# Cache pages in visits of four with seven buffers, late weight chunks in two sets

## The chip, the cores and the metric

The kernel is one program on one core of a Trainium2 chip. The metric is the device time of one execution in microseconds (us), taken as the median of several runs. One more execution was run with the hardware profiler; every row that is quoted comes from it.

## The reference, cut to what matters

One inference step of a two-layer decoder, for a prompt of 512 tokens and for 8 samples of 8 new tokens each. Layer 0 is a gated delta rule. Then keys and values are projected once, and layer 1 is differential attention over them. The samples also attend to 1024 older tokens each, whose keys and values lie in a paged cache: 8 pages of 128 tokens a sample, so 64 pages of keys and 64 of values.

```python
k_past = cache_k[page_table].reshape(db, past, DIFF_HEADS, 2 * DIFF_DH)
v_past = cache_v[page_table].reshape(db, past, DIFF_HEADS, DIFF_VH)
...
s = jnp.einsum('bqhmd,bkhmd->bhmqk', q, k) * DIFF_DH ** -0.5
s = jnp.where((k_pos[None, :] <= q_pos[:, None])[None, None, None], s, -jnp.inf)
p = jax.nn.softmax(s, axis=-1)
p = p[:, :, 0] - lam * p[:, :, 1]
return jnp.einsum('bhqk,bkhe->bqhe', p, v)
...
o = rms_norm(o, sub_gain) * (1.0 - lam_init)
o = o * jax.nn.silu(z.astype(F32)).reshape(b, L, DIFF_HEADS, DIFF_VH)
return o.reshape(b, L, DIFF_WIDTH).astype(h.dtype) @ w_out
```

## The kernel before, in words

The second half of the program (`phase_b`) holds layer 0's closing projection, then the projections q, k, v and z of layer 1 and the shared keys and values, the attention of prompt and samples, and the closing projection of layer 1. All 576 tokens (512 of the prompt, 64 of the samples) are columns, in two halves of 288.

**Weights.** A projection goes by chunks of 128 output rows: chunks 0 to 7 close layer 0, 8 to 15 are q, 16 to 23 k, 24 to 31 v, 32 to 39 z, 40 to 47 close layer 1. A chunk is loaded as it is (`raw`, two buffers, line 2003, on SyncE's queue) and split (`split_w`) into a rounded part `hi`, copied by ScalarE (line 2018), and a rest `lo`, subtracted in two halves by GpSimd (line 2024; half of it by VectorE for chunks 8 to 19). A chunk's half takes 24 matmuls: hi times the high part of the input, hi times its low part, lo times its high part, for 8 slices of the contraction (`run_part`). A pair hi and lo is a weight set; its room is named. Chunks up to 23 use room `w` (four sets), chunk 26 room `wx`, the other late ones `w2`: two sets, and a third from the point `late` on, when the buffers that k and q needed are given up. A set is freed behind the last matmul of its chunk's second half. In `tile_row` the first two tiles of k and z and the last two of every kind go half by half in turn (tile 6 half 0, tile 7 half 0, tile 6 half 1, tile 7 half 1); the others go one chunk after the other.

**Cache pages.** `Pages.loads` brings the 128 pages in one fixed order (keys of samples 0 to 2, then values of sample 0, keys of 3, values of 1, and so on) into a ring of `PG` = 5 buffers, 512 KB each. For each, GpSimd copies the page's number into the buffer (line 2478) once the buffer is free, SyncE reads it from there (line 2481) and issues the transfer (line 2483). `Sample2.keys` and `Sample2.values` are the users: TensorE multiplies two pages at a visit, in the form 128x32 (four column strips of the array, 16 instructions a page in the records). A half of the keys' scores (4 pages) lies in one PSUM buffer, and is copied out before the next half; the values of 8 pages add up in another. Between keys and values of a sample stands its softmax.

**The order.** A planner (`Second.drive`) writes the order of every engine while the program is built. Each piece of work is a generator with a rank; each of its steps names an engine, a cost, and what it waits for. The planner takes the step that can start first, and among equals the lowest rank: split 4, page loads 9, samples 20 to 27, prompt heads 29 and 30, projections 1000. So the projections fill TensorE where nothing else is ready. It has its own clock for the engines and the transfers. A buffer that is left inside a step counts as free at the end of that step:

```python
            for where, name in self.later:
                where[name] = end
```

The order so found is pinned for TensorE, ScalarE, VectorE, GpSimd and SyncE (`pin`): on the chip each engine takes its instructions in just this order, and waits where data are not there.

**The end.** `samples_end` joins the samples' results when all pages are done: four TensorE steps with small steps of VectorE, ScalarE and GpSimd between, then the gate with z (`gated2`). `out_second` closes layer 1: its first four half chunks are run for seven of eight slices (`HELD`), then their last slices, then the other twelve. Half 0 needs the prompt's heads alone, half 1 the samples too.

Of the kernel before, what the change touches and what calls it, by code (L numbers as in the profile page):

```python
# [10 lines left out]
F32 = mybir.dt.float32  # L11
# [17 lines left out]
NPG = 8  # L29
# [841 lines left out]
PG = 5  # L871
# [18 lines left out]
PAGES_AT = 1, 7  # L890
HELD = 4
EV = 3
CH = 3
PB = 3

# [1087 lines left out]
def act(n, k=0):  # L1983
    return 0.155 + 0.00086 * n + 0.1 * (k > 0) + 0.195 * (k > 1)
# [10 lines left out]
def weights(W, K, first, n, slot):  # L1995


    for j in range(first, first + n):
        room = "w" if j < 24 else "wx" if j == 26 and EV > 2 else "w2"
        yield None, 0, Room("raw")  # L2000
        rr, = W.took
        raw = K.wraw.tile([128, 8, 128], F32, name="wraw")
        K.nc.sync.dma_start(out=raw[:], in_=K.wall[K.worder[K.wnext + j]].rearrange("p (k m) -> p k m", m=128))
        if j <= 2:
            W.done[("raw", j)] = 0.0, None
        else:
            W.load("S", 1.5, "raw", j)
        W.add(4, split_w(W, K, j, raw, rr, room, slot[room]))


def split_w(W, K, j, raw, rr, room, slot):
    nc = K.nc
    yield "A", act(1024), ("raw", j), Room(room), *((("wa", j - 1),) if j - 1 in W.sets and j > 1 else ())
    took, = W.took
    phi, plo = slot(took[1])
    hi = phi.tile([128, 8, 128], F32R, name="whi")
    lo = plo.tile([128, 8, 128], F32R, name="wlo")
    nc.scalar.copy(out=hi[:], in_=raw[:])  # L2018
    W.sets[j] = hi, lo, took
    W.set("wa", j)  # L2020
    for q in range(0, 8, 4):
        shared = q and HALF[0] <= j < HALF[1]
        yield ("S", dve(512)) if shared else ("P", pool_op(512))
        (nc.vector if shared else nc.gpsimd).tensor_sub(out=lo[:, q:q + 4], in0=raw[:, q:q + 4], in1=hi[:, q:q + 4].bitcast(F32))  # L2024
    W.leave(rr)
    W.set("w", j)
# [320 lines left out]
def second_projections(W, K):  # L2347
# [40 lines left out]
    for i, (m, half) in enumerate(order):  # L2388
        if i < 3:
            bank = early[i][2]  # L2390
            yield from run_part(W, K, m, bank[0], half, (6, 7), conds=heads_in)
        else:
            yield from one(m, m, half, "o", nothing)
            bank = W.done_bank
        if half:
            W.leave(W.sets[m][2])
        yield None, 0, ("xl", half, m)
        W.add(0, first_out(W, K, m, m, half, xs[half, m][0], bank, xs[half, m][1]))
        if (m, half) == (7, 0):
            W.add(-6, second_norm(W, K, 0))  # L2400
        if (m, half) == (7, 1):
            W.add(-6, second_norm(W, K, 1))
# [12 lines left out]
            yield from run_part(W, K, 8 + t.h, bank[0], 1, (k,), conds=conds[1])  # L2415
    for t, bank in zip(tiles, banks):
        W.add(0, t.evac(1, bank))
        W.leave(W.sets[8 + t.h][2])
# [17 lines left out]
def tile_row(W, K, tiles, j, kind, conds, first=0):  # L2436


    order = [(t, half) for t in tiles[first:6] for half in range(2)]
    if kind in "kz":  # L2440
        order = [(t, half) for half in range(2) for t in tiles[:2]] + order[4:]
    order += [(t, half) for half in range(2) for t in tiles[6:]]
    for t, half in order:
        name = "pp" if kind in "qk" or t.h < EV and kind == "v" else "pq"
        if kind == "v" and t.h == EV and half == 0:
            yield None, 0, ("late",)
        yield from take(W, K, pick(W, "pq", "pt2", "sc", "pv") if kind == "z" and ("pv", 7, 3) in W.done else name)
        bank, = W.out
        yield from run_part(W, K, j + t.h, bank[0], half, range(8), conds=conds[half])
        W.add(0, t.evac(half, bank))  # L2450
        if half:
            W.leave(W.sets[j + t.h][2])
            if j + t.h in (20, 21, 22):
                W.leave(("w2", j + t.h - 20) if j + t.h < 22 else ("wx", 0))
        if t.h == 7:
            W.set(kind + "p", half)


class Pages:


    def __init__(self, W, K):
        self.W, self.K = W, K
        self.tiles = {}
        self.order = [("k", b) for b in range(PB)]
        for b in range(NB):
            self.order += [("v", b)] + ([("k", b + PB)] if b + PB < NB else [])

    def loads(self):
        W, K, P = self.W, self.K, self.W.P  # L2470
        nc = K.nc
        for kind, b in self.order:
            for pg in range(NPG):
                yield "Q", 0.2, Room("pg"), ("ptt",), ("sq", *PAGES_AT)
                i = b * NPG + pg
                t = K.pg.tile([128, 8, 128], F32, name="pg")
                e = t[0:1, 0, 0:1].bitcast(I32)
                nc.gpsimd.tensor_copy(out=e, in_=P.ptt[0:1, i:i + 1])  # L2478
# [4 lines left out]
                nc.sync.dma_start(out=t[:], in_=cache[bass.ds(r, 1)].rearrange("a p (h t) -> p (a h) t", h=8))  # L2483
                W.load("S", 1.55, kind + "page", i)


class Sample2:
# [5 lines left out]
    def keys(self):  # L2493
# [12 lines left out]
        p = self.p = P.sp.tile([128, 1088], F32, name="sp", bufs=PB)  # L2506
        nc.gpsimd.memset(p[:, 1024:], NEG)
        for half in range(2):
            for pair in range(2):
                ids = [b * NPG + 4 * half + 2 * pair + i for i in range(2)]  # L2510
                yield "E", None, *[("kpage", i) for i in ids], *((Room("px"),) if pair == 0 else ())
                if pair == 0:
                    sr, = W.took
                    S = K.px.tile([128, 512], F32, name="px")
                for n, i in enumerate(ids):
                    kp, kr = self.G.tiles["k", i]
                    o = 128 * (2 * pair + n)
# [65 lines left out]
    def values(self):  # L2583
        W, K, P, b = self.W, self.K, self.W.P, self.b
        nc = K.nc
        for pair in range(4):
            ids = [b * NPG + 2 * pair + i for i in range(2)]
            yield "E", None, *[("vpage", i) for i in ids], *((Room("po"),) if pair == 0 else ())
            if pair == 0:
                por, = W.took  # L2590
                po = K.po.tile([128, 4, 128], F32, name="po")
            for n, i in enumerate(ids):
                vp, vr = self.G.tiles["v", i]
                pg = 2 * pair + n
                for hf in range(2):
                    for j in range(4):
                        h = 4 * hf + j
# [19 lines left out]
def samples_end(W, K):  # L2617
# [11 lines left out]
    W.leave(xr)  # L2629
    yield "A", 0.65, Room("pg")  # L2630
    r0, = W.took
    sq = K.pg.tile([128, 8, 128], F32, name="pg")[:].rearrange("p a b -> p (a b)")[:, 0:512]
# [156 lines left out]
def out_second(W, K):  # L2789
# [40 lines left out]
    for (m, half), bank in zip(order[:HELD], held):  # L2830
        yield from run_part(W, K, 40 + m, bank[0], half, (7,), conds=conds(half))
        W.add(0, evac(m, half, bank))
        if half:
            W.leave(W.sets[40 + m][2])
    for i, (m, half) in enumerate(order[HELD:]):
        name = names[(i + HELD) % 8]
        yield None, 0, Room(name)
# [1 line left out]
        yield from run_part(W, K, 40 + m, bank[0], half, range(8), conds=conds(half))  # L2839
        W.add(0, evac(m, half, bank))  # L2840
        if half:
            W.leave(W.sets[40 + m][2])


def ada_later_loads(W, K, kts, bufs, ns, at):
# [117 lines left out]
def phase_b(K, ctx, past):  # L2963
# [41 lines left out]
    W.taken["w2"], W.taken["wx"] = 3, 1  # L3005
    W.sets[0] = *K.wq.pop(0), ("w", 0)
    W.done[("w", 0)] = max(0.0, past.done[("w", past.last)][0] - past.free["E"]), None
    own = K.whi, K.wlo
    pages = Pages(W, K)
# [3 lines left out]
    slot = {"w": lambda i: own if i % 4 < 2 else qx, "w2": lambda i: own if i % 3 < 2 else P.third, "wx": lambda i: qx}  # L3013
# [196 lines left out]
```

## Time and profile before

| | us |
|---|---|
| median of 3 runs | 1165.18 |
| lowest, highest run | 1161.04, 1165.52 |
| time of the profiled execution | 1162.21 |
| its span, first to last instruction | 1160.5 |
| TensorE busy | 1131.4 |
| VectorE, ScalarE, GpSimd busy | 690.6, 692.3, 437.7 |

The profiled execution's own time is 1.7 us above its span. TensorE appears as PE (matmuls) and PEld (weight loads), VectorE as DVE, ScalarE as ACT, GpSimd as POOL, SyncE as SP. A matmul's row begins when it starts; rows of matmuls that follow each other overlap, so the distance from start to start tells what one costs, not its own length. A row `x32` is 32 instructions of one kind in a run.

### The profile page before, as it was taken

How to read it: one execution, taken by the hardware profiler on the slowest of the kernel's cores; microseconds unless marked ns; L12 is line 12 of the kernel's file. 1: busy time of each engine (PE TensorE's matmuls, PEld its weight loads, DVE VectorE, ACT ScalarE, POOL GpSimd, SP SyncE). 2: the span in 40 equal slices, each digit the busy share in tenths (PEclk: the TensorE clock that was granted, in tenths of full speed). 3: DMA queues.
4: the chain of work that ended last, by engine and by line, in shares of the span. 5: the costliest groups of instructions: out<-in, count | busy, mean ns of one | idle time of the engine just before them, and what ended most of it. 6: DMA issues, size and time to landing. Idle time of an engine off the chain costs nothing.

```text
span 1160.5 us, 32592 instructions
## 1 busy us (share of the span) xinstructions
PE 1131.4 (97%) x12715; PEld 1039.0 (90%) x12715; DVE 690.6 (60%) x1739; ACT 692.3 (60%) x1901; POOL 437.7 (38%) x752
## 2 busy tenths in 40 slices
PE   8999999999999999999999999999999999999998
PEld 6899998989989998998989999999997887778998
DVE  4677875767877674866743757574424445554342
ACT  3675867777777767676653334775535656555320
POOL 3443434233333333232223431579933232233341
PEclk8999999999999999999999999999999999999999
DMA  9796666757657665676885888222689989898243
GB/s 365 207 230 167 147 193 134 201 146 201 167 153 171 157 199 134 190 204 149 244 248 157 304 274 322 92 74 75 231 290 309 313 310 303 300 320 282 63 137 110
DMA packets 87643, 239.96 MB, mean 207 GB/s; under 512 B 14451, under 2 KB 28659, under 8 KB 87491
## 3 DMA queue, kind: packets, MB, share of 16 engines
q1 hardware_dynamic: 71938, 181.27, 46.0%
q0 software_dynamic: 15552, 56.63, 22.4%
q8 instruction: 100, 1.64, 0.6%
q14 instruction: 53, 0.43, 0.1%
HBM read 212.02 MB, written 25.84 MB: 205 GB/s over the span
## 4 chain that ended last, share of the span: by engine, by line
PE 80%; DMA 6%; ACT 5%; issue 3%; DVE 3%; POOL 2%; SPq 0%; POOLq 0%; ACTq 0%; DVEq 0%
PE pp L271 23%; PE pp L1927 14%; PE pc L271 7%; PE pq L1927 6%; PE px L1927 4%; PE pa L271 3%; PE po L1927 3%; DMA whi<-wall 3%; PE pt L271 3%; PE sc L1927 3%; PE pt L1927 3%; PE pt L1932 3%; PE pv L1927 2%; PE ps L271 2%; PE pt L285 1%
## 5 line engine op out<-in xcount | busy, mean ns | idle before, releaser
L271 PE MATMUL pp<-hlo,whi 128*128 128x288 f32 x592 | 170.7, 310 | 0.0
L271 PE MATMUL pp<-hhi,whi 128*128 128x288 f32 x592 | 162.0, 295 | 0.0
L2024 POOL TENSOR_TENSOR wlo<-wraw,whi 128x512 fp32r<-128x512 f32 x82 | 110.1, 1359 | 113.1 <-ACT whi L2018 104.9
L1927 PE MATMUL pp<-hhi,whi 128*128 128x288 f32 x432 | 133.2, 309 | 0.7 <-DVE x L1826 0.7
L1927 PE MATMUL pp<-hlo,whi 128*128 128x288 f32 x432 | 127.3, 295 | 0.0
L1927 PE MATMUL pp<-hhi,wlo 128*128 128x288 f32 x432 | 125.8, 295 | 0.0
L271 PE MATMUL pp<-hhi,wraw 128*128 128x288 f32 x576 | 124.1, 299 | 0.0
L271 PEld LDWEIGHTS pp<-hlo,whi 128*128 128x128 f32 x592 | 111.6, 189 | 1.8 <-issue 1.4
L271 PEld LDWEIGHTS pp<-hhi,whi 128*128 128x128 f32 x592 | 111.7, 189 | 0.4
L271 PE MATMUL pp<-hhi,wlo 128*128 128x288 f32 x592 | 104.1, 304 | 0.0
L271 PEld LDWEIGHTS pp<-hhi,wraw 128*128 128x128 f32 x576 | 94.4, 189 | 1.0 <-issue 0.4
L1131 DVE SCALAR_TENSOR_TENSOR y<-u,vec,y 128x600 f32<-128x600 f32 x96 | 80.9, 842 | 10.8 <-ACT y L1128 10.2
L1927 PEld LDWEIGHTS pp<-hhi,whi 128*128 128x128 f32 x432 | 81.5, 189 | 5.2 <-issue 4.7
L271 PEld LDWEIGHTS pp<-hhi,wlo 128*128 128x128 f32 x592 | 85.1, 190 | 0.8 <-issue 0.2
L2478 POOL COPY pg<-ptt 1x1 int32<-1x1 int32 x128 | 27.5, 222 | 154.0 <-PE px L1927 67.8
L271 PE MATMUL pp<-hlo,wraw 128*128 128x288 f32 x288 | 84.7, 316 | 0.2 <-DVE hlo L1852 0.2
L1927 PEld LDWEIGHTS pp<-hlo,whi 128*128 128x128 f32 x432 | 81.6, 189 | 0.0
L1927 PEld LDWEIGHTS pp<-hhi,wlo 128*128 128x128 f32 x432 | 80.9, 189 | 0.0
L923 POOL DMA_DIRECT2D wlo<-wall x36 | 32.2, 895 | 122.4 <-ACT wlo L918 80.9
L2018 ACT CAST whi<-wraw 128x1024 fp32r<-128x1024 f32 x47 | 49.0, 1047 | 40.0 <-DMA wraw<-wall 20.1
L1927 PE MATMUL pq<-hhi,whi 128*128 128x288 f32 x192 | 61.9, 322 | 1.6 <-DVE x L2230 1.0
L1927 PE MATMUL pq<-hhi,wlo 128*128 128x288 f32 x192 | 56.7, 295 | 0.0
(483 smaller groups left out, 3135.5 us busy)
## 6 DMA issues: line engine op xcount, KB each, us to landing
pg<-ck SPq DMA_DIRECT2D x64, 512.0 KB, 5.1
pg<-cv SPq DMA_DIRECT2D x64, 512.0 KB, 4.9
wraw<-wall SPq DMA_DIRECT2D x49, 512.0 KB, 4.3
wraw<-wall POOLq DMA_DIRECT2D x36, 512.0 KB, 5.9
whi<-wall POOLq DMA_DIRECT2D x36, 512.0 KB, 5.8
wlo<-wall POOLq DMA_DIRECT2D x36, 512.0 KB, 5.7
araw<-ada SPq DMA_DIRECT2D x24, 512.0 KB, 4.3
araw<-ada SPq DMA_DIRECT2D x8, 1024.0 KB, 13.2
```

Source lines behind the costliest of these rows:

```text
L271: return self.K.nc.tensor.matmul(**kw)
L285: return self.K.nc.tensor.transpose(**kw)
L923: K.nc.gpsimd.dma_start(out=lo[:], in_=src, accum_op=ALU.add)
L1131: nc.vector.scalar_tensor_tensor(out=y[:, :YW], in0=u[:, j:j + YW], scalar=cw[j], in1=y[:, :YW], op0=ALU.mult, op1=ALU.add)
L1927: return self.K.nc.tensor.matmul(**kw)
L1932: return self.K.nc.tensor.transpose(**kw)
L2018: nc.scalar.copy(out=hi[:], in_=raw[:])
L2024: (nc.vector if shared else nc.gpsimd).tensor_sub(out=lo[:, q:q + 4], in0=raw[:, q:q + 4], in1=hi[:, q:q + 4].bitcast(F32))
L2478: nc.gpsimd.tensor_copy(out=e, in_=P.ptt[0:1, i:i + 1])
```

## The change

Samples from the fourth on (`b >= PB`) take four pages of keys at a visit in place of two, and all samples take four pages of values. The ring of page buffers has five places up to the point `late` and seven after it: two more (`MORE`) in a pool of their own, `bpg2`, which lies where the third weight set lay. That set is gone, so late chunks have two. Chunk 40, the first of the closing projection, has its set in two page buffers: its split waits for all page loads to be issued (`loads`) and for two free places of the ring. `Pages.tile` finds the pool to which a place of the ring belongs. Since chunks after 40 skip one turn in `w2`, 41 takes the set of 38 and 42 that of 39.

```diff
+BURST = 4
+MORE = 2
+OVER = 40,
...
-        room = "w" if j < 24 else "wx" if j == 26 and EV > 2 else "w2"
+        room = "w" if j < 24 else "wx" if j == 26 and EV > 2 else "pg" if j in OVER else "w2"
...
 def split_w(W, K, j, raw, rr, room, slot):
     nc = K.nc
-    yield "A", act(1024), ("raw", j), Room(room), *((("wa", j - 1),) if j - 1 in W.sets and j > 1 else ())
-    took, = W.took
-    phi, plo = slot(took[1])
-    hi = phi.tile([128, 8, 128], F32R, name="whi")
-    lo = plo.tile([128, 8, 128], F32R, name="wlo")
+    yield ("A", act(1024), ("raw", j), *((Room(room),) if slot else (Room(room), Room(room), ("loads",))),
+           *((("wa", j - 1),) if j - 1 in W.sets and j > 1 else ()))
+    took = W.took
+    if slot:
+        phi, plo = slot(took[0][1])
+        hi = phi.tile([128, 8, 128], F32R, name="whi")
+        lo = plo.tile([128, 8, 128], F32R, name="wlo")
+    else:
+        hi, lo = (W.pages.tile(r)[:].bitcast(F32R) for r in W.took)
...
+    def tile(self, room):
+        n = room[1] - self.grown
+        pool = self.K.pg2 if n >= 0 and n % (PG + MORE) < MORE else self.K.pg
+        return pool.tile([128, 8, 128], F32, name="pg")
...
         for half in range(2):
-            for pair in range(2):
-                ids = [b * NPG + 4 * half + 2 * pair + i for i in range(2)]
+            many = BURST if b >= PB else 2
+            for pair in range(4 // many):
+                ids = [b * NPG + 4 * half + many * pair + i for i in range(many)]
...
-        for pair in range(4):
-            ids = [b * NPG + 2 * pair + i for i in range(2)]
+        for pair in range(NPG // BURST):
+            ids = [b * NPG + BURST * pair + i for i in range(BURST)]
...
-                       ("w", 4), ("w2", 3), ("wx", 1), ("qs", 2), ("p", PB), ("pTs", 1), ("os", 1), ("C", 2), ("ls", 2), ("mx", 2),
+                       ("w", 4), ("w2", 2), ("wx", 1), ("qs", 2), ("p", PB), ("pTs", 1), ("os", 1), ("C", 2), ("ls", 2), ("mx", 2),
...
-    P.third = [pool(n, 1) for n in ("bwh", "bwl")]
-    W.done[("late",)] = W.left["w2", 2] = W.now, None
+    K.pg2 = pool("bpg2", MORE)
+    pages.grown = W.taken["pg"]
+    W.bufs["pg"] += MORE
+    W.done[("late",)] = W.now, None
```

More of the change, by code (lines that the diff above doesn't have):

```diff
@@ L2395, in second_projections @@
         if half:
-            W.leave(W.sets[m][2])
+            W.leave(*W.sets[m][2])
         yield None, 0, ("xl", half, m)
@@ L2451, in tile_row @@
         if half:
-            W.leave(W.sets[j + t.h][2])
+            W.leave(*W.sets[j + t.h][2])
             if j + t.h in (20, 21, 22):
@@ L2463, in __init__ @@
         self.W, self.K = W, K
-        self.tiles = {}
+        self.tiles, self.grown = {}, math.inf
         self.order = [("k", b) for b in range(PB)]
@@ L2484, in loads @@
                 W.load("S", 1.55, kind + "page", i)
+        W.set("loads")
 class Sample2:
@@ L2516, in keys @@
                     kp, kr = self.G.tiles["k", i]
-                    o = 128 * (2 * pair + n)
+                    o = 128 * (many * pair + n)
                     for hh in range(2):
@@ L2833, in out_second @@
         if half:
-            W.leave(W.sets[40 + m][2])
+            W.leave(*W.sets[40 + m][2])
     for i, (m, half) in enumerate(order[HELD:]):
@@ L2841, in out_second @@
         if half:
-            W.leave(W.sets[40 + m][2])
+            W.leave(*W.sets[40 + m][2])
 def ada_later_loads(W, K, kts, bufs, ns, at):
@@ L3004, in phase_b @@
     W.taken["pg"] = W.taken["w"] = 1
-    W.taken["w2"], W.taken["wx"] = 3, 1
-    W.sets[0] = *K.wq.pop(0), ("w", 0)
+    W.taken["w2"], W.taken["wx"] = 2, 1
+    W.sets[0] = *K.wq.pop(0), [("w", 0)]
     W.done[("w", 0)] = max(0.0, past.done[("w", past.last)][0] - past.free["E"]), None
     own = K.whi, K.wlo
-    pages = Pages(W, K)
+    pages = W.pages = Pages(W, K)
     samples = [Sample2(W, K, pages, b) for b in range(NB)]
@@ L3012, in phase_b @@
     W.add(7, set_up(W, K, one))
-    slot = {"w": lambda i: own if i % 4 < 2 else qx, "w2": lambda i: own if i % 3 < 2 else P.third, "wx": lambda i: qx}
+    slot = {"w": lambda i: own if i % 4 < 2 else qx, "w2": lambda i: own, "wx": lambda i: qx}
     W.add(3, weights(W, K, 1, 47, slot))
```

10 lines of the change are left out of this document (5 added, 5 removed).

## The prediction

> **What bounds the kernel now.** I read the shares of the page first, then TensorE's own waits, then the timeline around single page visits, the ring of page buffers, and last the chain of waits behind the last page.
>
> ```profile
> span 1160.5 us, 32592 instructions
> PE 1131.4 (97%) x12715; PEld 1039.0 (90%) x12715; DVE 690.6 (60%) x1739; ACT 692.3 (60%) x1901; POOL 437.7 (38%) x752
> ...
> PE px L1927 <- DMA pg<-ck: 1.4, 1, 1.4
> ...
> PE po L1927 <- POOL pg L2478: 0.8, 2, 0.4
> ...
> PE po L1927 <- DMA pg<-cv: 0.2, 1, 0.2
> ...
> 893.00:1077.00 184.00, 181.09 (x2575) 148.92 (x2575) 92.91 (x239) 107.75 (x315) 53.99 (x137) 1.00 0.88 301
> ...
> 893.00:1077.00 184.00, 52.72 (x1536) 38.86 (x1536) 0.00 (x0) 0.00 (x0) 19.05 (x91) 1.00 0.88 301
> ```
>
> TensorE is the bound, and nearly never idle. In its stretch of page visits, 893 to 1077 us, it is busy for 181.09 of 184 us at full clock; the last row counts there what touches pages alone: 1536 matmuls of 32 a visit, so 48 visits. All that TensorE loses on pages in the whole program is 1.4 + 0.8 + 0.2 = 2.4 us. So time can be won only where TensorE's work gets shorter, and lost only where it runs out of work.
>
> **A visit's price, and the edit to fours.**
>
> ```profile
> 1067.38 0.29 PE L1927 MATMUL pq<-hlo,whi 128*128 128x288 f32 x1
> 1067.51 0.29 PE L1927 MATMUL pq<-hhi,wlo 128*128 128x288 f32 x1
> 1067.74 1.08 PE L1927 MATMUL po<-pg,pTs 128*32 128x128 f32 x32
> 1068.75 0.40 PE L1927 MATMUL pq<-hhi,whi 128*128 128x288 f32 x1
> 1068.99 0.29 PE L1927 MATMUL pq<-hlo,whi 128*128 128x288 f32 x1
> ...
> 939.52 1.08 PE L1927 MATMUL po<-pg,pTs 128*32 128x128 f32 x32
> 940.42 0.41 PE L1927 MATMUL px<-kT,qs 128*32 128x64 f32 x16
> ...
> 984.10 0.64 PE L1932 MATMUL px<-con_ident,sp 128*128 128x128 f32 x4
> 984.67 1.08 PE L1927 MATMUL px<-pg,qs 128*32 128x128 f32 x32
> ...
> 1044.38 0.66 PE L1932 MATMUL px<-con_ident,sp 128*128 128x128 f32 x4
> 1044.88 1.06 PE L1927 MATMUL pv<-vn,pts 128*128 128x128 f32 x8
> ```
>
> Projection matmuls start 0.13 us apart (1067.38, 1067.51). Into a visit it is 0.23, from its start to the next matmul 1.01, and that one's successor starts 0.24 later. So a visit between projection matmuls costs 0.23 + 1.01 + 0.24 - 2 x 0.13 = 1.22 us. Where work of the same form follows, as at 939.52, the same 32 take 0.90. A second pair that joins the first therefore saves 0.32 us. Between transposes it saves less: four of them take 0.57 ahead of a visit against 0.50 ahead of a 128x128 matmul, which leaves 0.07 + (1.01 - 0.90) = 0.18. Keys of five samples drop from 4 visits to 2, values of eight from 4 to 2: 10 + 16 = 26 visits fewer, 26 x 0.18 = 4.7 to 26 x 0.32 = 8.3 us. Both neighbours are common; I take 0.25 each, **6.5 us**. Matmuls, page copies on POOL and page transfers keep their number.
>
> [...]
>
> **Seven buffers: the ring, and what the planner makes of it.**
>
> ```profile
> POOL pg L2478 <- PE px L1927: 67.8, 41, 5.7
> POOL pg L2478 <- PE po L1927: 55.4, 40, 5.8
> ...
> 928.89 1.08 PE L1927 MATMUL px<-pg,qs 128*32 128x128 f32 x32
> 932.27 1.08 PE L1927 MATMUL px<-pg,qs 128*32 128x128 f32 x32
> 936.43 1.08 PE L1927 MATMUL px<-pg,qs 128*32 128x128 f32 x32
> ...
> 929.69 0.17 POOL L2478 COPY pg<-ptt 1x1 int32<-1x1 int32 x1 [4.16 <-PE px L1927]
> ...
> pg<-ck SPq DMA_DIRECT2D x64, 512.0 KB, 5.1
> ```
>
> 81 of the 128 copies of page numbers wait for a buffer, so the ring sets the pace of the pages. One turn: the visit at 928.89 frees its first buffer, the copy runs at 929.69, the transfer takes 5.1 from issue to landing, and that page is the second one of the visit at 936.43, two visits and 7.54 us later. On average four pages take 184 / 24 = 7.67 us. With five buffers in pairs three pages are under way when a visit starts, and the page that comes first from the visit's own buffers completes the visit after next: four pages a turn. With seven in fours three are under way again, and the first freed buffer completes the very next visit: also four pages a turn. The two extra buffers buy nothing in pace. But the order is written by the planner, which counts all buffers of a step as free at the step's end, and a step of four pages is 0.90 longer. So a turn becomes about 7.67 + 0.90 = 8.57 us in the pinned order. The chip itself frees each page behind its own matmuls, so bounds are 0 (the order does not shift) and, for burst effects that no row shows, as much as 1.3 a turn. I take 0.9: 24 turns from the second half of sample 0's values to the last give **+21.6 us** for the end of the page stream.
>
> Against it stands the point `late`:
>
> ```profile
> 878.35 1.11 PE L1927 MATMUL po<-pg,pTs 128*32 128x128 f32 x32
> ...
> 888.53 1.08 PE L1927 MATMUL po<-pg,pTs 128*32 128x128 f32 x32
> ...
> 875.84 4.99 POOL L2024 TENSOR_TENSOR wlo<-wraw,whi 128x512 fp32r<-128x512 f32 x4 [2.18 <-ACT whi L2018]
> 880.77 0.62 POOL L2478 COPY pg<-ptt 1x1 int32<-1x1 int32 x4
> ```
>
> Two visits lie 10.2 us apart there, 6.3 more than 7.67 / 2: four subtractions for chunks 27 and 28, which waited for the third set and its neighbours, sit ahead of four page copies on POOL, and SP issues raw chunks among the pages. Without a third set chunk 27 is split when 24 is done, well before. I give back 5 of the 6.3 (bounds 0 and 10, two pages more in flight), and the 2.4 us of page waits, since pages then land earlier than the order needs them. TensorE also finds chunk 27 ready sooner: 0.5 us.
>
> **The tail decides.**
>
> ```profile
> 1076.00 0.78 PE po L1927 x31
> ...
> 1087.99 0.89 PE px L1927 x8
> ...
> 1100.01 3.21 PE pq L1927 x24
> ...
> 1106.26 2.09 DVE hlo L2670 x2
> ...
> 1108.39 5.69 PE px L1927 x41
> ```
>
> Now the last page matmul ends at 1076.8, the samples' last TensorE step (1087.99) at 1088.9, z at 1103.2, and 1108.4 is the start of the closing projection's first half that needs the samples: 5.2 behind z for the gate, hi and lo. Everything behind 1108.4 is solid matmuls.
> - TensorE's side after the change: z ends at 1103.2 - 6.5 - 2.4 - 0.5 = 1093.8, the half could start at 1099.0.
> - The pages' side: the stream ends at 1076.8 + 21.6 - 5 - 2.4 = 1091.0. From there to the last TensorE step it took 12.1 with projections between; with less of them 10, and 3 more for the steps of DVE and ACT behind it: 1104.0.
>
> The later one counts: 1108.4 - 1104.0 = **4.4 us won**, the rest of the saving is idle time ahead of the closing projection. The profiled execution took 1162.2, so 1157.8; the runs' median is 3.0 above that execution, which gives 1160.8. I forecast between the two, **1159**.
>
> **Two sets, and chunk 40.**
>
> ```profile
> 1131.23 1.05 ACT L2018 CAST whi<-wraw 128x1024 fp32r<-128x1024 f32 x1 [4.04 <-PE pv L1927]
> ...
> 1132.35 2.54 POOL L2024 TENSOR_TENSOR wlo<-wraw,whi 128x512 fp32r<-128x512 f32 x2 [2.55 <-ACT whi L2018]
> ...
> 1131.19 3.16 PE pq L1927 x24
> ...
> 1066.72 3.21 SPq L2483 DMA_DIRECT2D pg<-cv  x3
> ```
>
> A split that waits for its set takes from 1131.2 to 1134.9, 3.7 us, while a half chunk takes 3.2 and a chunk 6.4. One after the other, the set in use hides the split. Where tiles alternate by halves 0.5 is left: chunks 31, 34 and 39, at most 1.5 us together, and visits and heads fill it; I cost it at nothing. Behind a late cast on ACT stand the heads' exponentials, on POOL the page copies; they would go late by the same 0.5. Raw chunks stay as many on SP's queue, only longer in their buffers. Chunk 40 waits for the last page issue, now at 1069.9 and so 6.9 us ahead of the stream's end, hence 1084; its 3.7 end before z at 1093.8. Without that cover it costs 3.7.
>
> **Rivals.**
> - *TensorE's side decides* (the order does not shift, or by under 0.7 a turn): 9.4 us won, 1152.8 by the profiled execution, about 1154 in the median. For it: buffers do come free page by page. Against: the order is pinned.
> - *The page stream outlasts the projections* (slower): z is eaten up while pages are still due, then TensorE idles between visits. It turns to a loss from a stream end of 1095.4 on (13 ahead of 1108.4), 4.4 later than forecast, a turn of 8.75. At 1.3 a turn it is 9.6 later, 5.2 us lost: 1167.4 to 1170. For it: four transfers are then issued in one burst; against: 2.4 us of waits go away.
> - *Two sets do not keep up*: if each of the 13 late chunks from 35 on is short by 0.5, 6.5 us of TensorE's saving goes, its side comes to 1105.5, and about 3 us are left: 1162.
> [...]
>
> **Chances.** Forecast 0.40, TensorE's side 0.25, stream outlasts 0.15, two sets 0.20. What can be told from no change is 0.5%, 5.8 us. Faster by more: half of the first, nearly all of the second, a fifth of the last, 0.48. Slower by more: most of the third, little else, 0.14. Within: 0.38. The range 1151 to 1168 takes the full 9.4 from the lower runs, and the loss of the third case at its likelier end.
>
> **What would show it.** 38 page visits, 26 of them of 64 matmuls; 8.4 to 8.8 us from one to the next; the last page matmul near 1091; little z left behind it; a gap on TensorE of some 5 us ahead of the first half that needs the samples. The step is wrong if that gap is missing (then it is faster), if the visits keep 7.7 us a turn, or if TensorE waits on ACT or POOL for late weight sets.

## The result, and the profile after

| | before | changed |
|---|---|---|
| median of 5 runs, us | 1165.18 | 1154.02 |
| lowest to highest, us | 1160.89 to 1169.27 | 1152.23 to 1154.72 |
| profiled execution, us | 1162.21 | 1154.71 |

The changed kernel takes 0.991 of the time, with a 95% interval of 0.989 to 0.994: some 10 us less. The forecast was 1159, within 1151 to 1168. The time lies inside the range, but the forecast's own mechanism, a page stream that comes late and eats half of the saving, did not happen. What happened is the rival "TensorE's side decides" (chance 0.25), for which the prediction had "1152.8 by the profiled execution, about 1154 in the median". That the median meets the 1154 is in part luck: the profiled execution took 1154.71, 7.5 us less than before and not 9.4, while the median before happens to lie 3.0 above its profiled execution and the one after 0.7 below. Of all runs reported here two took some 2140 us, one of them of e12 below: the ratios leave them out, and e12's median without it is 1150.69 and not 1151.64.

The page of the changed kernel, its two first lines:

```profile
span 1152.9 us, 32576 instructions
...
PE 1122.2 (97%) x12715; PEld 1038.4 (90%) x12715; DVE 690.8 (60%) x1739; ACT 691.7 (60%) x1901; POOL 436.7 (38%) x752
```

The number of TensorE's instructions is unchanged, its busy time is 9.2 us less: 6.9 us of this lie behind the first page matmul (measured below), the rest ahead of it, where the code is the same in both. Next the timeline of TensorE (start, duration, and what ran): the visit that ends sample 0's values, and the last visit of all.

```profile
884.65 1.96 PE L1930 MATMUL po<-pg,pTs 128*32 128x128 f32 x64
...
1072.76 1.95 PE L1930 MATMUL po<-pg,pTs 128*32 128x128 f32 x64
1074.64 0.40 PE L1930 MATMUL pq<-hhi,whi 128*128 128x288 f32 x1
```

64 matmuls a visit as intended, and the last page matmul ends at 1074.7: 2 us earlier than before, where the prediction had 1091. There are 38 visits. The two windows are the rows of the prediction again, for all work and for pages alone.

```profile
893.00:1077.00 184.00, 181.77 (x2587) 155.70 (x2580) 96.06 (x239) 107.08 (x317) 54.72 (x138) 1.00 0.86 297
...
893.00:1077.00 184.00, 45.48 (x1492) 1.00 0.86 297
```

TensorE remains the bound, with 181.77 of 184 us busy, and its page work has fallen from 52.72 to 45.48 us, most of it by the shorter visits (44 page instructions now lie ahead of this window). TensorE's waits (what was waited for, us in total, times, longest) no longer hold one for a page (a second trace of this kernel has one of 0.4). Of those behind the first visit the one that grew most is for a step of VectorE, the first row here, which was 1.0 us before:

```profile
PE pq L1930 <- DVE x L2237: 2.4, 3, 1.1
...
PE px L1930 <- DVE hlo L2684: 1.0, 1, 1.0
```

The chain of waits behind the last page (start, duration, what), and the one wait of TensorE there in its timeline:

```profile
1072.83 1.88 PE po L1930 x64
...
1086.31 0.89 PE px L1930 x8
...
1092.42 3.21 PE pq L1930 x24
1095.63 0.02 issue
...
1098.67 2.10 DVE hlo L2684 x2
...
1100.81 5.67 PE px L1930 x41
```

```profile
1100.81 0.40 PE L1930 MATMUL px<-hlo,pg 128*128 128x288 f32 x1 [0.97 <-DVE hlo L2684]
```

z ends at 1095.63 where it was 1103.2, and the half that needs the samples runs on at 1100.81 where it was 1108.39 (its second matmul, the first that needs `hlo`; a first one with `hhi` is done ahead of it). That is 7.6 us, the whole difference of the two spans (1160.5 and 1152.9). The idle time ahead of it is 0.97 us, as before (1.0), and not the 5 us of the forecast.

### The profile page after: what moved, and what is told of

It is laid out like the page before. It is cut to its first block, busy times and chain, and to the rows that moved or that the text cites. A ratio compares the mean times of both kernels' runs of the same rounds, so it can differ in the third digit from the quotient of the medians.

```text
span 1152.9 us, 32576 instructions
## 1 busy us (share of the span) xinstructions
PE 1122.2 (97%) x12715; PEld 1038.4 (90%) x12715; DVE 690.8 (60%) x1739; ACT 691.7 (60%) x1901; POOL 436.7 (38%) x752
## 4 chain that ended last, share of the span: by engine, by line
PE 76%; ACT 8%; DMA 6%; DVE 4%; issue 4%; POOL 1%; SPq 0%; ACTq 0%; POOLq 0%; DVEq 0%
PE pp L271 23%; PE pp L1930 12%; PE pc L271 7%; PE pq L1930 7%; PE px L1930 4%; PE po L1930 3%; PE sc L1930 3%; PE pt L1935 3%; PE pa L271 3%; PE pt L271 3%; PE pt L1930 2%; PE pv L1930 2%; PE ps L271 2%; DMA araw<-ada 2%; PE pt L285 1%
## 5 line engine op out<-in xcount | busy, mean ns | idle before, releaser
L1930 PE MATMUL pq<-hlo,whi 128*128 128x288 f32 x200 | 58.9, 295 | 0.0
```

Of the source, the lines that this page charges most:

```text
L1930: return self.K.nc.tensor.matmul(**kw)
```

## The experiments

Traces differ ahead of the page visits, where the code is the same for all kernels: the first page matmul starts anywhere from 809.1 to 815.0 us. So besides the medians I compare the traces from that matmul on, to the end of the last matmul: the phase. Each row gives the window, its length, TensorE's busy time, the other engines, and then the granted clock, the DMA share and GB/s; the first is of the kernel before, the second of the changed one.

```profile
813.39:1156.63 343.24, 337.20 (x4163) 294.80 (x4162) 149.97 (x356) 162.19 (x422) 124.81 (x245) 1.00 0.74 250
```

```profile
813.52:1149.08 335.56, 330.34 (x4163) 295.44 (x4162) 150.60 (x356) 160.44 (x422) 123.13 (x245) 1.00 0.75 255
```

The phase lasts 343.24 and 335.56 us. TensorE's work in it fell by 6.86 us, and its idle time (length less busy time) from 6.04 to 5.22. A second trace of the changed kernel, taken beside the last experiments, gives 335.99 with 330.36 busy, though its first page matmul starts at 810.65 in place of 813.52. From this one repeat I take 0.5 us as what the phase can tell; the experiments ran on three chips, and no other kernel was traced twice.

All times in this table are in us, counted from the first page matmul. A turn is four pages: the time from the last matmul of the 32nd page (sample 0's values) to the last one of the 128th, divided by 24. "Last page" is the start of that last matmul. "Half" is the second matmul of the closing projection's first half that needs the samples. Busy is TensorE's in the phase. The ratio is to the kernel before, measured beside the run.

| kernel | pages a visit, ring | turn | last page | half | phase | busy | median, ratio with interval |
|---|---|---|---|---|---|---|---|
| before | 2, 5 | 7.80 | 263.1 | 295.0 | 343.2 | 337.2 | 1165.18 |
| changed | 4, 7 | 7.84 | 260.9 | 287.3 | 335.6 | 330.3 | 1154.02, 0.991 (0.989 to 0.994) |
| e3 | 2, 7 | 6.44 | 225.1 | 290.1 | 338.4 | 334.9 | 1155.83, 0.993 (0.991 to 0.996) |
| e2 | 4, 6 | 9.10 | 292.3 | 305.0 | 354.6 | 339.3 | 1173.26, 1.008 (1.005 to 1.011) |
| e1 | 4, 5 | 9.90 | 317.6 | 333.0 | 383.6 | 353.0 | 1201.35, 1.031 (1.028 to 1.034) |
| e10 | 4, 6, by page | 8.12 | 267.6 | 287.5 | 335.8 | 330.6 | 1155.22, 0.995 (0.993 to 0.997) |
| e11 | 4, 7, by page | 6.84 | 235.2 | 286.3 | 334.6 | 329.3 | 1152.93, 0.993 (0.990 to 0.995) |
| e13 | 2, 5, by page | 7.61 | 252.2 | 296.7 | 345.0 | 336.6 | 1165.46, 1.002 (0.999 to 1.004) |
| e4 | 2, 5 | 7.63 | 254.8 | 295.0 | 345.9 | 337.9 | 1163.03, 1.000 (0.998 to 1.002) |
| e5 | 4, 7 | 7.84 | 261.1 | 287.5 | 338.3 | 331.2 | 1156.44, 0.996 (0.994 to 0.998) |
| e6 | 1, 5 | 7.22 | 242.9 | 309.0 | 357.2 | 346.9 | 1175.54, 1.014 (1.010 to 1.018) |
| e9 | 4, 7, fewer visits | 8.00 | 274.1 | 287.4 | 337.0 | 329.0 | 1155.45, 0.995 (0.994 to 0.997) |
| e12 | e9, by page | 7.14 | 249.0 | 282.4 | 330.7 | 325.7 | 1151.64, 0.990 (0.986 to 0.993) |
| changed again | 4, 7 | 7.84 | 261.3 | 287.7 | 336.0 | 330.4 | 1152.80, 0.993 (0.991 to 0.995) |

### Visits of two, with all the rest of the change (e3)

```diff
-BURST = 4
+BURST = 2
```

> The changed kernel with visits of two again: seven buffers, two weight sets, chunk 40 in page buffers, 64 visits; nothing of the computation is left out. Theory (most of the gain is the 26 visits that TensorE is spared, the rest the 2.4 us of page waits): the page waits go, the visits cost what they cost before, so 2 to 3 us less than the kernel before, 1162 to 1163 beside a median of 1165; TensorE's busy time is that of the kernel before, 1131, and not 1122. Rival (the gain comes from the two buffers, through the late point and the page waits): most of the 7.6 us that the closing projection starts earlier is there without visits of four, 1155 to 1158. Rival (the two sets and chunk 40 in page buffers cost, hidden in the change by other savings): 1165 to 1169.

The window of this kernel from its first page matmul on:

```profile
811.16:1149.52 338.36, 334.94 (x4163) 294.32 (x4162) 147.31 (x356) 162.02 (x422) 123.48 (x245) 1.00 0.72 253
```

The theory was wrong about the split. Most of the gain is there without visits of four: the phase falls from 343.24 to 338.36, 4.9 of 7.7 us, and the ratio can't be told from that of the whole change. Of the 4.9, 2.6 are idle time (6.04 to 3.42), where the 2.4 us of page waits went, and 2.3 are work. The work is less though visits are nearly as many (62 runs of page matmuls in place of 64): TensorE changes its matmul form (the rows and columns of the array that a matmul uses, as 128x128 or 128x32) 177 times in the phase and not 184, counted between matmuls that follow each other; by the price measured below, 0.15 each, that is 1 us. The other 1.3 us I can't place. The order alone may move TensorE's work by that much: e11 below has 139 changes of form where the changed kernel has 138, and its work is 1.0 us less (329.31 and 330.34). Four at a visit then bring 2.8 us more: 4.6 less work, 1.8 more idle. That is 0.19 for each of the 24 visits saved on top of e3, and 0.12 for each of 39 changes of form.

Buffers, sets and chunk 40's place, without visits of four, also move the page stream, which ends 38 us earlier (225.1 after the first visit, before 263.1) and by that wins nothing: the half still starts where TensorE's own work lets it.

### A ring of five and of six (e1, e2)

Visits of four on the old ring with the third weight set kept (e1), and the change with one more buffer in place of two (e2):

```diff
-OVER = 40,
+OVER = ()
...
-                       ("w", 4), ("w2", 2), ("wx", 1), ("qs", 2), ("p", PB), ("pTs", 1), ("os", 1), ("C", 2), ("ls", 2), ("mx", 2),
+                       ("w", 4), ("w2", 3), ("wx", 1), ("qs", 2), ("p", PB), ("pTs", 1), ("os", 1), ("C", 2), ("ls", 2), ("mx", 2),
...
-    K.pg2 = pool("bpg2", MORE)
-    pages.grown = W.taken["pg"]
-    W.bufs["pg"] += MORE
-    W.done[("late",)] = W.now, None
+    P.third = [pool(n, 1) for n in ("bwh", "bwl")]
+    W.done[("late",)] = W.left["w2", 2] = W.now, None
```

```diff
-MORE = 2
+MORE = 1
```

> Visits of four alone: the ring stays at five buffers and the third weight set stays, chunk 40 has its own set; nothing of the computation is left out. Theory (TensorE's work sets the end as long as the page stream keeps ahead of it; in the changed kernel the stream ends at 1074.7 and the first half that needs the samples starts at 1100.8, so with the 13 us that the prediction put between the two the stream has about 13 us to spare): with five buffers only one page is under way when a visit of four starts, and the third page that it frees completes the next visit, where with seven the first one does. Two page numbers more a turn, each 0.5 (page spacing in a visit) to 1.6 us (page copy, issue and landing one after the other), so a turn of 8.9 to 11 in place of 7.9; over 24 turns the stream ends 25 to 75 us later, and with 13 to spare the time is 1165 to 1215, with waits for pages on TensorE of more than 12 us. Rival (TensorE alone decides, wherever the stream ends): 26 visits fewer, the saving of 6.5 us less the 2 us of page waits: 1156 to 1159. Rival (the visits of four bring nothing, the two buffers do): 1163 to 1166, waits as before.

> The changed kernel with one buffer more after the point late in place of two, a ring of six; nothing of the computation is left out. Theory (TensorE's work sets the end, the page stream has about 13 us to spare): the second freed page completes the next visit, one page number more a turn, 0.5 to 1.6 us, a turn of 8.4 to 9.5; over 24 turns the stream ends 12 to 38 us later than at 1074.7, so 1087 to 1113. Up to 1088 nothing is lost, beyond it each us is: 1153 to 1179, likeliest 1165. If the loss begins before the stream's end reaches 1088, the 13 us between stream and closing projection are too few; if the end is beyond 1095 and nothing is lost, they are too many. Rival (TensorE alone decides): 1153 to 1155.

Both came out as the theory had it: turns of 9.10 and 9.90, times of 1173 and 1201. Here the page stream does set the end. In e2 its last visit and the chain behind it read:

```profile
1102.75 2.21 PE L1930 MATMUL po<-pg,pTs 128*32 128x128 f32 x64
...
1109.58 1.36 PE L1930 MATMUL px<-ones,pg 128*128 128x1 f32 x8 [1.49 <-ACT pg L2647]
1112.27 2.08 PE L1930 MATMUL px<-con_ident,rny 128*128 128x128 f32 x8 [1.34 <-POOL rny L167]
1116.65 0.61 PE L1930 MATMUL px<-hhi,pg 128*128 128x288 f32 x1 [2.30 <-ACT hhi L2682]
```

```profile
1112.27 2.09 PE px L1930 x8
...
1116.63 0.70 DVE hlo L2684
...
1117.37 7.04 PE px L1930 x41
```

No projection is left to cover the joining steps, and TensorE waits for each. From the start of the last page matmul (1104.7) to the half it takes 12.7 us; 15.4 in e1. The prediction had 13. In the changed kernel the same distance is 26.4, and so 13 to 14 us are to spare.

### The planner's count, page by page (e10, e11, e13)

The prediction's lost step rested on a rule of the planner: buffers left inside a step count as free at its end. These three kernels change that count alone, for e2's ring of six, for the changed kernel, and for the kernel before. Instructions stay the same, their order may shift.

```diff
             self.now, self.cost, self.later, self.rank, self.took, self.use = x, cost or 0.0, [], w[0], [], 0.0
+            self.early = []
...
             for where, name in self.later:
                 where[name] = end
+            for name, share in self.early:
+                self.left[name] = x + self.cost * share, eng
...
-                    W.leave(kr)
+                    W.early.append((kr, (n + 1) / many))
...
-                W.leave(vr)
+                W.early.append((vr, (n + 1) / BURST))
```

> The kernel with fours and a ring of six (which took 1173.3 us, turn of four pages 9.09, stream end 1104.7), but the planner counts each page buffer of a visit as free after its own share of the visit, and not at the visit's end; the chip's instructions stay the same, only their order may change; nothing of the computation is left out. Theory of the prediction (the planner's counting at the step's end sets the turn in the pinned order): the second page of a visit is counted free 0.95 us earlier, the turn falls to 8.1 to 8.3, over 24 turns the stream ends some 20 us earlier, near 1085, TensorE's side decides: 1153 to 1157. Theory now (what counts is how many transfers are under way when a visit starts, on the chip; the planner's counting moves little): turn 8.9 to 9.1, 1169 to 1174.

> The changed kernel (fours, ring of seven), but the planner counts each page buffer of a visit as free after its own share of the visit; the instructions stay the same, only their order may change; nothing of the computation is left out. With six buffers this took the turn from 9.09 to 8.12. Theory (the planner's count delays the page that completes the next visit: with seven the first of the four, 1.9 us of visit less its own 0.48, so 1.4; the prediction's step was right in kind, and its base wrong, since seven in fours would be faster than five in pairs): the turn falls from 7.84 to between 6.4 and 7.0, the stream ends 20 to 34 us earlier, near 1050, and the time stays, as TensorE's side decides: 1152 to 1155. Rival (with seven the count costs nothing, the turn is the chip's own): the turn stays at 7.7 to 7.9, same time.

> The kernel before (pairs, ring of five) with the planner's count page by page; the instructions stay the same, only their order may change; nothing of the computation is left out. Theory (the count delays the decisive page, here the first of a pair, by half a visit, 0.48): the turn of four pages falls from 7.80 to 7.3 or so, the stream ends 12 us earlier, near 1065, and the time stays within 3 us, since TensorE's side decided there too: 1161 to 1165. Rival (pairs are paced by the transfers alone): turn 7.7 to 7.9.

The row that groups all value pages (count; least, median and largest duration in ns; first and last start) for e2, e10 and e11 in this order:

```profile
L1930 PE MATMUL po<-pg,pTs x1024: 269/273/423, 875.6 to 1104.7; 128*32 128x128 f32 x171
```

```profile
L1930 PE MATMUL po<-pg,pTs x1024: 272/273/297, 872.1 to 1076.7; 128*32 128x128 f32 x171
```

```profile
L1930 PE MATMUL po<-pg,pTs x1024: 269/273/298, 875.9 to 1048.1; 128*32 128x128 f32 x171
```

With six buffers the turn falls from 9.10 to 8.12 and the phase by 18.8 us (354.6 to 335.8): the prediction's theory, against the one I held by then. With seven it falls from 7.84 to 6.84, and the time stays (0.993 beside 0.993 for the changed kernel measured with it), since TensorE's work sets the end. With pairs on five it falls by 0.19 only, from 7.80 to 7.61, less than the 0.5 expected. There TensorE's waits for values still on their way grow from 0.2 to 3.3 us:

```profile
PE po L1927 <- DMA pg<-cv: 3.3, 6, 0.8
```

So the order of the pairs could hardly be made tighter, since pages came late at once, while the order of the fours was looser than their ring by 1 us a turn. The rows between which a turn is counted, for the kernel before (whose first one the prediction shows), e11 and e13:

```profile
1075.70 1.08 PE L1927 MATMUL po<-pg,pTs 128*32 128x128 f32 x32
```

```profile
882.36 1.95 PE L1930 MATMUL po<-pg,pTs 128*32 128x128 f32 x64
...
1046.43 1.96 PE L1930 MATMUL po<-pg,pTs 128*32 128x128 f32 x64
```

```profile
884.24 0.64 PE L1927 MATMUL po<-pg,pTs 128*32 128x128 f32 x16 [0.38 <-DMA pg<-cv]
...
1066.35 1.08 PE L1927 MATMUL po<-pg,pTs 128*32 128x128 f32 x32
```

### Two weight sets, and chunk 40 (e4, e5)

The kernel before with two late sets (e4), and the changed kernel with chunk 40 in the late room again (e5):

```diff
-                       ("w", 4), ("w2", 3), ("wx", 1), ("qs", 2), ("p", PB), ("pTs", 1), ("os", 1), ("C", 2), ("ls", 2), ("mx", 2),
+                       ("w", 4), ("w2", 2), ("wx", 1), ("qs", 2), ("p", PB), ("pTs", 1), ("os", 1), ("C", 2), ("ls", 2), ("mx", 2),
...
-    slot = {"w": lambda i: own if i % 4 < 2 else qx, "w2": lambda i: own if i % 3 < 2 else P.third, "wx": lambda i: qx}
+    slot = {"w": lambda i: own if i % 4 < 2 else qx, "w2": lambda i: own, "wx": lambda i: qx}
...
-    P.third = [pool(n, 1) for n in ("bwh", "bwl")]
-    W.done[("late",)] = W.left["w2", 2] = W.now, None
+    W.done[("late",)] = W.now, None
```

```diff
-OVER = 40,
+OVER = ()
```

> The kernel before with two weight sets for the late chunks in place of three, all else as before (ring of five, visits of two, chunk 40 in the late room); nothing of the computation is left out. Theory (the third set bought nothing, the set in use hides the next split): within 1 us of the kernel before, 1164 to 1166. Theory of the late point: chunk 27 is split before late, so the four subtractions no longer stand ahead of page copies there and the two visits 10.2 us apart come closer by 3 to 5 us, with no gain in time, as the stream has time to spare. Rival (two sets do not keep up): 0.5 us for each of the 13 late chunks from 35 on, 6.5 us, 1171 to 1172, with waits of TensorE for ACT or POOL at the late weight sets.

> The changed kernel with chunk 40 in the late room w2 like its neighbours, so that 40 takes the set of 38, 41 that of 39 and 42 that of 40; nothing of the computation is left out. Theory (the page buffers for chunk 40 buy that two closing chunks are split ahead of z's end and a third soon after): 42 can be split only when 40 is done, 3.7 us before TensorE may start on it; it has 41 to work on meanwhile, two half chunks of 3.2 each, so nothing to 3 us is lost against the changed kernel: 1154 to 1157, and any loss shows as a wait of TensorE for ACT or POOL on a weight set behind the half that needs the samples. Rival (chunk 40 in page buffers costs, by its wait for the last page): up to 2 us faster than the changed kernel, 1152.

e4's time is that of the kernel before, so the 6.5 us of the rival are out. Its phase is 2.7 us longer all the same (345.9 and 343.2), though the half starts where it did. Its 32nd page ends 4.4 us earlier, 71.6 after the first visit in place of 76.0: the third set was what held the pages up at `late`. Behind `late`, both kernels show the same wait, e4's first and e5's second:

```profile
PE sc L1927 <- POOL wlo L2024: 1.4, 2, 0.8
```

```profile
PE sc L1930 <- POOL wlo L2031: 1.4, 2, 0.8
...
PE sc L1930 <- ACT whi L2025: 0.3, 1, 0.3
```

It stands in the closing projection, behind the first two half chunks that follow the samples; by the turn of the sets this is chunk 42, which is split into the set of 40 once 40 is done. In e5 the phase is 2.3 to 2.8 us longer than in the two traces of the changed kernel. The medians don't resolve this, the traces do. The two waits explain 1.7 us of it; TensorE's busy time is also 0.9 us more (331.2 and 330.3). So two sets cost nothing in the change because chunk 40 has its set elsewhere.

### One page at a visit (e6)

```diff
-            for pair in range(2):
-                ids = [b * NPG + 4 * half + 2 * pair + i for i in range(2)]
+            for pair in range(4):
+                ids = [b * NPG + 4 * half + pair]
...
-                    o = 128 * (2 * pair + n)
+                    o = 128 * (pair + n)
...
-        for pair in range(4):
-            ids = [b * NPG + 2 * pair + i for i in range(2)]
+        for pair in range(8):
+            ids = [b * NPG + pair]
...
-                pg = 2 * pair + n
+                pg = pair + n
```

> The kernel before with one page at a visit in place of two, ring of five, 128 visits; nothing of the computation is left out. Theory (each change of the matmul form costs 0.12 to 0.15 us: between the kernel before and the changed one TensorE's starts come 6.85 us closer together from the first page visit on, with 46 changes of form fewer; between the pairs with seven buffers and the changed kernel 4.6 us with 39 fewer): 64 visits more are up to 128 changes more, 15 to 19 us, less the 2.4 us of page waits, since four of five pages are then under way when a visit starts: 1176 to 1181; where late pages let visits run together, less: 1172. [...] Rival (visits cost nothing of their own; the gain came from the buffers alone): 1161 to 1164. The turn of four pages should fall from 7.80 to about 7, between the 7.80 with three pages under way and the 6.44 with five.

The median lies between the theory's two figures, and the turn is the 7 it gave. Late pages let visits run together, so there are 105 of them and not 128. TensorE's busy time in the phase:

```profile
811.54:1168.73 357.19, 346.91 (x4163) 293.22 (x4162) 147.60 (x356) 162.81 (x422) 124.83 (x245) 1.00 0.70 240
```

346.91 - 337.20 = 9.71 us for 41 more visits, 0.24 each; 63 changes of form more (247 in place of 184), 0.154 each. In the change, 46 fewer (138) go with 6.86 less, 0.149 each, but part of that came without visits of four (e3). The prediction took 0.25 a visit.

### Fewer visits still (e9, e12)

Keys of samples 0 to 2 in fours too, and, from sample 3 on, the short matmuls with the samples' own keys in the step of the second four (e9); the same with the count page by page (e12).

```diff
-            many = BURST if b >= PB else 2
+            many = BURST
...
+                own = b >= PB and half == 1
-                yield "E", None, *[("kpage", i) for i in ids], *((Room("px"),) if pair == 0 else ())
+                yield ("E", None, *[("kpage", i) for i in ids], *((Room("px"),) if pair == 0 else ()),
+                       *((Room("px"), *[("k", h) for h in range(8)]) if own else ()))
...
+                if own:
+                    self.own = W.took[1], self.own_keys(qs)
```

> The changed kernel with 11 visits fewer: the keys of samples 0 to 2 also come in fours, 6 visits fewer, and from sample 3 on the 16 short matmuls with the samples' own new keys are done in the same TensorE step as the second four pages of keys, so 5 changes into the form 128x32 and back are saved; nothing of the computation is left out. Theory (TensorE's work sets the end, a visit saves 0.25): 2 to 3 us less than the changed kernel, 1151 to 1152 beside 1154. Rival (the fours of samples 0 to 2, which still run on five buffers, put the page stream back: a turn of 9.9 as with fours on five buffers throughout, six turns): these 12 visits now take 55.7 us, 9.3 for four pages, so 4 us later at most, and the stream, ending 12 to 13 us before it would count, hides it; no change to that of the theory. Rival (the second room for scores, taken early, holds up the prompt's heads): 1154 to 1156.

> The kernel with 11 visits fewer (e9: keys of samples 0 to 2 in fours too, own keys in the step of the second four) with the planner's count page by page; nothing of the computation is left out. e9's page stream ended at 1084.5, 13.05 before the half that needs the samples, so the pages' side decided there and TensorE's saving was lost to waits behind the last page. Theory: with a turn of 7 the stream ends 20 us earlier, TensorE's side decides again and the 11 visits' 2.75 us show: from the first page visit to the last matmul 332 to 333 in place of the changed kernel's 335.6, 1150 to 1152 beside 1153 to 1155 of the changed kernel in the same call. Rival (the fours on five buffers at the start put the stream back too far, or the short matmuls' early room costs): no gain, 1154 to 1157.

> The changed kernel itself, beside the others of this call on the same chip, as their reference: 0.991 of the kernel before (0.989 to 0.994), so 1151 to 1155; from the first page visit to the last matmul 335.6, the same order and the same turn of 7.84. What differs from the first profile lies ahead of the first page visit.

32 visits. e9 brings nothing: 337.0 in the phase, the changed kernel 335.6 and 336.0. Its chain ends on the samples' side:

```profile
1092.44 2.09 PE px L1930 x8
...
1096.80 0.70 DVE hlo L2696
...
1097.55 7.02 PE px L1930 x41
```

The fours on five buffers delay the first samples, so that the 32nd page ends 9.2 us later than in the changed kernel and the last one 13.2 (274.1 in place of 260.9), 13.3 ahead of the half. The other 4 us come behind the 32nd page, where the turn is 8.00 in place of 7.84; whether the short matmuls in the step of the second four do this was not tested. The rival that the expectation had priced at "4 us later at most" was three times as large and used up what the stream had to spare. With the count page by page the last page is back at 249.0 and the saved visits show, 3.9 us against e11, whose count is the same:

```profile
811.15:1141.87 330.72, 325.73 (x4163) 295.68 (x4162) 151.35 (x356) 161.91 (x422) 124.02 (x245) 1.00 0.75 259
```

330.7 us from the first page matmul to the last matmul, 4.9 less than the changed kernel's 335.6 and 12.5 less than before. Its median, 1151.64, and its ratio of 0.990 (0.986 to 0.993) are the lowest here, but the interval overlaps that of the changed kernel measured beside it (0.991 to 0.995). So that it beats the changed kernel is what two traces show, and the medians leave it open.

## Why the prediction was right and wrong, step by step

- **TensorE is the bound: right.** In all kernels but e1, e2 and e9, the half starts when TensorE's own work and the 5.2 us behind z allow it.
- **A visit costs 0.25: right in size, but the sum was met in part by luck.** Predicted 6.5 us less work for 26 visits; 6.86 were measured. But 2.3 of these are there in e3, with 62 visits still. Fours on top of e3 save 0.19 a visit, and e6 gives 0.24 from the other side; at these prices 26 visits are worth 5.0 to 6.2 us.
- **The two extra buffers "buy nothing in pace", and a turn becomes 8.57: wrong, the step that failed.** The turn is 7.84, the stream ends at 1074.7 and not at 1091.0. Of its two terms, the planner's count was right: 0.90 more a turn than in pairs predicted, 0.81 measured (1.00 with seven buffers by e11, 0.98 with six by e10, less the 0.19 that the pairs lose to it by e13). The other, put at 0, is -0.77: with the count page by page on both sides, fours on seven take 6.84 where pairs on five take 7.61. The prediction counted three pages under way at the start of a visit in both and called that the same pace. The two terms cancel, 0.81 - 0.77 = 0.04, which is 7.84 less 7.80. Why three pages under way carry more in one burst than in pairs no run shows, nor the burst effects for which the prediction allowed up to 1.3 a turn (the turn rose by 0.04). What the runs show is that one page fewer under way costs 1.3 (e10 against e11).
- **The late point: right in kind.** Predicted 5 of the 6.3 us; the 32nd page is done 3.1 us earlier in the changed kernel, 4.4 in e4, 5.3 in e3. What makes 5.3 in pairs (e3) and 3.1 in fours no run takes apart.
- **13 us from the last page to the half: right**, 12.7 in e2 and 13.3 in e9, 15.4 in e1. The rival "page stream outlasts the projections" is real, and begins where it was put. It was one buffer away: e2 is the kernel that it described, with a turn 1.3 longer than before, at 1173 beside its 1167 to 1170.
- **TensorE's side, 9.4 us: in size 1.7 too much.** From the first page matmul to z's end 289.8 became 282.1, 7.7 less. Work gave 6.9 (6.5 predicted), idle time 0.8, where 2.4 for page waits and 0.5 for chunk 27 were predicted. The page waits did go; a longer wait for VectorE (1.0 to 2.4 us) and smaller ones came in their place.
- **Two sets and chunk 40 cost nothing: right, but only together.** The prediction gave each its own cover. In e5 chunk 40's place turns out to be the cover of the two sets, worth 2.3 to 2.8 us; e4, two sets without it, has a phase 2.7 us longer than before.
- **The gap of 5 us ahead of the closing half** was the sign to look for, and the prediction named its absence as what would prove the step wrong. It is 0.97 us.

What the prediction did not see is how much the change brings without visits of four: 4.9 us (e3), of which it had 2.9. Since the two parts overlap, 4.9 and 6.9 don't add up to 7.7: four at a visit on top of the buffers bring 2.8.

## What to carry to other kernels

When an order is pinned, find the pace that the plan allows and the pace that the buffers allow, and see which one is slower; a resource that is freed too late in the plan can cost nearly as much as one that is missing (here 1.0 and 1.3 us a turn). A ring's pace is not told by counting transfers under way at one moment (three by the count in e13 and in e11, at 7.61 and 6.84 us a turn): change the ring by one on each side and measure, for the end may be one buffer away from being set by it (e2, with one buffer less, took 1173.26 us). And where one engine bounds the whole, as TensorE does here, a faster stream is worth nothing by itself (e11: a turn 1.0 shorter, the ratio 0.993 beside 0.993), but its slack is what lets that engine's work be cut further (e12 against e9: the phase 330.7 and 337.0).

## What was not expected of the hardware

In e2 the granted clock of TensorE falls behind short waits. No wait of TensorE in this part is longer than 2.3 us; the granted clock (the third number from the end in these windows) goes down to 0.59 and 0.55, and is 0.76 in the last window, where TensorE is busy for 6.88 of 7 us:

```profile
1086.00:1092.00 6.00, 5.07 (x111) 4.04 (x110) 4.51 (x14) 4.30 (x13) 2.54 (x6) 1.00 0.94 313
1092.00:1098.00 6.00, 2.95 (x36) 1.81 (x34) 0.00 (x0) 1.04 (x1) 0.88 (x2) 0.59 0.97 337
1098.00:1104.00 6.00, 5.39 (x52) 5.08 (x56) 0.00 (x0) 1.05 (x1) 1.79 (x2) 0.55 0.80 298
...
1117.00:1124.00 7.00, 6.88 (x41) 6.63 (x41) 0.32 (x1) 0.00 (x0) 0.00 (x0) 0.76 0.00 0
```

The 41 matmuls of the half take 7.04 us in e2, 7.02 in e9 (granted clock 0.75 from 1097 to 1104) and 5.67 in the changed kernel (1.00 from 1100.8 to 1106.5), so a stream that comes late costs 1.4 us there on top of the wait. The busy times of e1, e2 and e9 in the table hold such stretches (granted clock over the phase 0.92, 0.97 and 0.98, where it is 1.00 in the kernel before and the changed one), and can't be compared with the others as work alone. From 1092 to 1098 in e2 the longest wait is 1.8 us, two of them leave TensorE busy for 2.95 of 6 us, and the clock is 0.59. What sets the clock there was not taken apart by any run. The two rows with the waits there:

```profile
1093.84 1.08 PE L1930 MATMUL po<-pg,pTs 128*32 128x128 f32 x16 [1.82 <-DMA pg<-cv]
1095.97 1.08 PE L1930 MATMUL po<-pg,pTs 128*32 128x128 f32 x16 [1.05 <-DMA pg<-cv]
```
